# Layer 0's first projections in stages of 128, 128, 256 and three of 512 features; the filter's loads behind a partial sum

## The chip, the cores and the metric

One Trainium2 chip, one core. The time is that of the device from start to end of one execution, in microseconds (us). Before the change it is 1778.45 us, the median of three runs (1774.54 to 1780.24).

## The reference, cut to what matters

A two-layer network over 256 context and 256 latent tokens of width 2048, batch 1, in float32. The part that the change touches is the head of layer 0:

```
mod_l = silu(c) @ ada_w[i] + ada_b[i]            # c: 2048, ada_w[i]: 2048 x 6144
mod_c = silu(c_ctx) @ ada_w[i] + ada_b[i]
sh, sc, gt = split(mod, 3)
h = rmsnorm(x, norm_w[i]) * (1 + sc) + sh        # 512 tokens x 2048 features
p = h @ w_in[i]                                  # 2048 x 6688
...                                              # S5, Hyena, retention and GLA branches of p
x = x + gt * (concat(gated branches) @ w_out[i])
```

The Hyena branch also needs a filter that hangs on no token: a small network of three sine layers over 256 positions, times a last weight (`hy_w4`), times a decay, and its transform. After both layers the latent tokens are normed once more and are the output.

## The kernel before, in words

Tokens lie along the free axis: a feature block of 128 is one tile of 128 partitions x 512 tokens. `h` cannot be formed for a feature before its shift and scale are there, and these need all 2048 rows of two columns of `ada_w`, 16.8 MB a section. So layer 0's first 2048 output columns (the inputs of S5, and queries and keys of GLA and retention: eight *units* of 256 columns) are summed in stages over the input features. `STAGES` holds the stages' bounds, in units of 256 features: two of 256, three of 512. In `layer0_qk` (L1298) stage f first makes its `h` tiles (`make_h`, each in a rounded part `hi` and a rest `lo`), and starts the modulation of the next stage as a background generator (`self.bg`, from `ada_feat` and `ada`). Then each unit loads its weights (`wpart` L966: one DMA of 256 rows x 256 columns into a `raw` buffer, a cast on ScalarE to `whi`, a subtraction on VectorE to `wlo`), does 12 matmuls (3 for each of 2 row blocks and 2 column halves, `proj_part` L990) and takes `steps` steps of the background. Stage 0 copies a unit's two sums out of PSUM to `part[n, j]` (ScalarE), later stages add to them (VectorE).

`ada` (L1071) computes both modulations at once. Its stationary operand `sc` has 32 columns, two of them in use, so each result takes 32 of TensorE's 128 columns, and four results stand side by side in PSUM tile `pa`: two sections by two halves of the block (`w = n // 2`, L1076). A DMA of 256 KB brings `nk` row blocks of one section; matmuls are issued after each load in stage 0 and after every fourth load (`GRP0`) else. Each fp32 matmul shows as two instructions in the trace. When all are in, `ada_cols` (L1101) transposes them to columns and adds the bias.

`hy_kf` (L488) makes the filter. Its seven larger loads (four parts of `w4`, two of `dec`, one `kd`) go through SP's queue; the small network's weights go through POOL's queue, its input `hyz` through ScalarE's (`const2` L166). `between` (L1490) runs it ahead of stage 1's units, and S5's loads, parameters and first generated part (`EG`) ahead of stages 2, 3 and 4.

Buffers: nine `raw` of 256 KB, shared by weights and ada loads; six each of `whi` and `wlo`; three PSUM banks `pj` and two `pB`, which units use in turn. A planner sets the order of instructions on each engine ahead of time from its own modelled timeline: what is written later may be issued earlier, and each engine then keeps that order.

Of the kernel before, what the change touches and what calls it, by code (L numbers as in the profile page):

```python
# [10 lines left out]
F32 = mybir.dt.float32  # L11
# [84 lines left out]

STAGES = (0, 1, 2, 4, 6, 8)
GRP, GRP0 = 4, 4
ENG = {'p': 'pp', 'm': 'pv', 'v': 'vv'}
HOW = 'tvtvtvtv'  # L100
# [5 lines left out]
ELF = 9  # L106
EG = (4, 9)
MARK = lambda label: None
# [8 lines left out]
class Net:  # L117
# [370 lines left out]
    def hy_kf(self, i, kfd):  # L488
# [4 lines left out]
        mark(f'hykf{i}')  # L493
        w4 = [self.t2() for _ in range(2)]
        for o in range(2):
            for d in range(2):
                nc.sync.dma_start(w4[o][d * 64:(d + 1) * 64], I['hy_w4'][i][:, (2 * d + o) * 512:(2 * d + o + 1) * 512])
        dec = [self.t2() for _ in range(2)]
        for jt in range(2):
            nc.sync.dma_start(dec[jt], self.C['hydec'][:, jt])  # L500
        kd = self.t2()
        nc.sync.dma_start(kd, self.C['kdft'].rearrange("p a b c -> p (a b c)"))
# [7 lines left out]
        for o in range(2):  # L510
            mark(f'hykf{i}')
            f = {}
# [21 lines left out]
            for ri in range(2):  # L534
                ps = []
# [429 lines left out]

    def wpart(self, src, r0, c0, w, step=True, keep=False):  # L966

        raw = self.raw()[:, :, :w]
        self.nc.sync.dma_start(raw, src[r0:r0 + 256, c0:c0 + w].rearrange("(k p) c -> p k c", p=128))
        if keep:  # L970
            hi, lo = (self.tp.tile([128, 2, 256], F32R, name="m" + t, tag="m" + t, bufs=NM[t])[:, :, :w] for t in 'AB')
        else:
            hi, lo = self.whl('whi')[:, :, :w], self.whl('wlo')[:, :, :w]
        self.nw += 1
        next(self.extra, None)
        self.split(hi, lo, raw, 'v')
        if step:
            self.due += self.rate
            n = int(self.due)
            self.due -= n  # L980
            self.step(n)
        return hi, lo
# [6 lines left out]

    def proj_part(self, W, kq, c0, ps, t0, first, last, step=True):  # L990

        hi, lo = self.wpart(W, kq * 256, c0, 256, step)
        for j in range(2):
            cs = slice(j * 128, (j + 1) * 128)
            o = ps[j][:, t0:]
            for k in range(2):
                xh, xl = self.hh[kq * 2 + k][:, t0:], self.hl[kq * 2 + k][:, t0:]
                self.mm(o, hi[:, k, cs], xh, start=first and k == 0, stop=False)
                self.mm(o, hi[:, k, cs], xl, start=False, stop=False)
                self.mm(o, lo[:, k, cs], xh, start=False, stop=last and k == 1)  # L1000

# [69 lines left out]
    def ada(self, i, cols, n, group, done):  # L1071
# [3 lines left out]
        nc = self.nc  # L1075
        w = n // 2  # L1076
        p = self.ps.tile([128, 512], F32, name="pa", tag="pa", bufs=1)[:, :w]
        src = self.I['ada_w'][i].rearrange("(p k) c -> p k c", k=KT)
# [4 lines left out]
        for m, (k, s, a) in enumerate(loads):  # L1083
# [3 lines left out]
            for dk in range(nk):  # L1087
                for b in range(0, wl, w):
                    todo.append((2 * s + (a + b) // w, k + dk, x[:, dk, b:b + w]))
            if (m + 1) % group == 0:  # L1090
# [3 lines left out]
            if m < len(loads) - 1:  # L1094
                yield
        r = self.sm.tile([128, 256], F32, name="adr", bufs=1)[:, :w]
        self.cp(r, p)
# [3 lines left out]
    def ada_cols(self, r, adab, k0, m):  # L1101

        n = r.shape[1] // 128
        p = self.ps.tile([128, 512], F32, name="pa", tag="pa", bufs=1)
        for s in range(n):
            self.tr(p[:, s * 128:(s + 1) * 128], r[:, s * 128:(s + 1) * 128])
# [191 lines left out]
    def layer0_qk(self, xT, m, adab, vec, rrow, between):  # L1298
# [4 lines left out]
        bounds = STAGES  # L1303
        stage = lambda f: self.ada_feat(0, bounds[f] * 256, (bounds[f + 1] - bounds[f]) * 256, m, adab, 1 if f == 0 else GRP0) \
            if f < ELF else self.ada_feat_el(0, bounds[f] * 256, m, adab, ELENG0)
# [3 lines left out]
        for f in range(last + 1):  # L1309
            kqs = range(bounds[f], bounds[f + 1])  # L1310
            for k in range(2 * kqs[0], 2 * kqs[-1] + 2):
                self.make_h(k, xT[k], m, vec, rrow)
            steps = 0
            if f < last:
                self.bg = stage(f + 1)
                steps = (bounds[f + 2] - bounds[f + 1]) * 16 // (len(units) * len(kqs)) + 1
            between(f)
            for n, (c0, j0, cb) in enumerate(units):
# [3 lines left out]
                mark(f'qk{f}')  # L1322
                for kq in kqs:
                    self.proj_part(W, kq, c0, ps, 0, kq == kqs[0], kq == kqs[-1], False)
                    self.step(steps)
                for j in range(2):
                    if f == 0:
                        part[n, j] = self.t2()
                        self.cp(part[n, j], ps[j])
                    else:  # L1330
                        self.add(part[n, j], part[n, j], ps[j])
                    if f == last:
                        cb(j0 + j, part[n, j])
# [122 lines left out]
    def run(self, out):  # L1456
# [33 lines left out]
        def between(f):  # L1490
            self.cur = 'A'
            if f == 1:
                for _ in hk:
                    pass
            if f == 2:
                self.s5_loads(0)
            if f == 3:
                Ps[0] = self.s5_params(0)
# [142 lines left out]
```

## Time and profile before

| | us |
|---|---|
| median of three runs | 1778.45 |
| the profiled execution | 1779.05 |
| its span in the profile | 1777.1 |
| TensorE (PE) busy | 1718.0, 97% |
| VectorE (DVE) busy | 1234.1, 69% |
| ScalarE (ACT) busy | 738.7, 42% |

The span runs from the first to the last instruction that the profiler saw; the execution's own time is 1.95 us longer. PE is the matmuls, whose ends are modelled: a busy PE need not be at its peak. SP is the engine that issues most DMAs and does nothing else; a `q` behind an engine's name stands for its sequencer, which waits or issues.

### The profile page before, as it was taken

To read this page: it belongs to the slowest core of one execution; us is meant where nothing else is said; L and a number is where in the kernel's file an instruction comes from. 1 tells how busy PE (TensorE), PEld (TensorE's weight loads), DVE (VectorE), ACT (ScalarE), POOL (GpSimd) and SP (SyncE) were. 2 spreads that over 40 slices of the span, in tenths; PEclk is the share of its full clock that TensorE was granted. 3 is DMA by queue.
4 is the path that set the end of the run, shared out by engine and by line. 5 is a ranking of instruction groups with operands and counts; after the bars stand their busy time and mean duration, and the time that the engine had idled before them with its cause. 6 is when DMAs were issued, how large, how long until landed. Compare 5 with 4: busy or idle time off the path is not lost.

```text
span 1777.1 us, 33615 instructions
## 1 busy us (share of the span) xinstructions
PE 1718.0 (97%) x12496; PEld 1403.8 (79%) x12496; DVE 1234.1 (69%) x2495; ACT 738.7 (42%) x1463; POOL 116.3 (7%) x184
## 2 busy tenths in 40 slices
PE   7999999999999999998999999999999999999997
PEld 4656678878777667875789889777997888899997
DVE  2464875569987695965698436558777788578864
ACT  4432253245345344231242433334355555454554
POOL 4000000000000000000023020000000000000133
PEclk9999999999999999999899999899999999999999
DMA  9776865557556486767785474549654435887963
GB/s 291 255 250 171 255 194 169 173 168 215 158 183 190 149 262 218 214 209 238 269 259 169 141 158 156 171 129 312 189 166 123 116 108 159 256 258 233 329 209 122
DMA packets 327995, 355.18 MB, mean 200 GB/s; under 512 B 62912, under 2 KB 247960, under 8 KB 327832
## 3 DMA queue, kind: packets, MB, share of 16 engines
q1 hardware_dynamic: 320672, 343.91, 63.5%
q10 hardware_dynamic: 5112, 8.79, 1.6%
q8 instruction: 98, 1.61, 0.4%
q0 software_dynamic: 2048, 0.34, 0.1%
q14 instruction: 65, 0.53, 0.1%
HBM read 316.11 MB, written 36.83 MB: 199 GB/s over the span
## 4 chain that ended last, share of the span: by engine, by line
PE 79%; DMA 10%; DVE 5%; ACT 2%; issue 2%; SPq 1%; POOL 0%; ACTq 0%; DVEq 0%
PE pj L199 34%; PE pj L1043 20%; PE pB L199 10%; PE pA L199 7%; PE pa L199 4%; DMA raw<-in_w_in_dram 3%; DMA raw<-in_ada_w_dram 2%; PE pB L203 2%; DVE mA L184 1%; PE pA L886 1%; DMA kd<-mA 1%; PE pB L1043 1%; DVE acc L196 1%; DVE wlo L184 1%; PE pA L203 1%
## 5 line engine op out<-in xcount | busy, mean ns | idle before, releaser
L199 PE MATMUL pj<-hs,whi 128*128 128x512 f32 (+1 forms) x2496 | 665.2, 354 | 3.3 <-ACT whi L957 3.1
L957 ACT CAST whi<-raw 128x512 fp32r<-128x512 f32 (+1 forms) x536 | 331.3, 621 | 677.9 <-DMA raw<-in_w_in_dram 298.5
L184 DVE TENSOR_TENSOR wlo<-raw,whi 128x512 fp32r<-128x512 f32 (+1 forms) x536 | 373.1, 702 | 276.6 <-ACT whi L957 259.6
L199 PEld LDWEIGHTS pj<-hs,whi 128*128 128x128 f32 x2496 | 430.0, 190 | 85.7 <-issue 19.3
L1043 PE MATMUL pj<-whi,hs 128*128 128x256 f32 (+1 forms) x2368 | 453.3, 288 | 0.5 <-ACT tr L1426 0.4
L199 PE MATMUL pj<-hs,wlo 128*128 128x512 f32 (+1 forms) x1248 | 439.8, 355 | 0.9 <-DVE wlo L184 0.9
L1043 PEld LDWEIGHTS pj<-whi,hs 128*128 128x128 f32 x2368 | 370.4, 189 | 22.1 <-issue 19.6
L1043 PE MATMUL pj<-wlo,hs 128*128 128x256 f32 (+1 forms) x1184 | 337.5, 285 | 0.0
L199 PEld LDWEIGHTS pj<-hs,wlo 128*128 128x128 f32 x1248 | 235.3, 189 | 43.1 <-issue 11.3
L1043 PEld LDWEIGHTS pj<-wlo,hs 128*128 128x128 f32 x1184 | 223.3, 189 | 5.0 <-issue 4.7
L184 DVE TENSOR_TENSOR mA<-mA 128x512 f32<-128x512 f32 (+6 forms) x342 | 180.8, 557 | 29.3 <-DMA mA<-rq 10.9
L196 DVE SCALAR_TENSOR_TENSOR acc<-raw,sc,acc 128x512 f32<-128x512 f32 x210 | 155.5, 762 | 8.1 <-DMA raw<-in_ada_w_dram 7.5
L199 PE MATMUL pA<-mA 128*64 128x64 f32 (+4 forms) x892 | 119.3, 298 | 5.5 <-DMA mA<-in_s_glu_w_dram 5.1
L199 PE MATMUL pa<-raw,sc 128*32 128x256 f32 (+1 forms) x1152 | 97.0, 371 | 7.6 <-DMA raw<-in_ada_w_dram 6.6
L199 PE MATMUL pB<-hs,whi 128*128 128x512 f32 x320 | 103.6, 403 | 0.1
L199 PE MATMUL pB<-mB 64*64 64x128 f32 (+4 forms) x896 | 95.3, 297 | 8.1 <-DVE mB L184 6.5
L199 PEld LDWEIGHTS pA<-mA 128*64 128x64 f32 (+2 forms) x892 | 75.1, 159 | 27.7 <-issue 15.5
L177 ACT COPY mA<-pA 128x512 f32<-128x512 f32 (+3 forms) x130 | 52.4, 427 | 85.5 <-PE pA L199 44.2
L199 PEld LDWEIGHTS pB<-mB 64*64 64x64 f32 (+2 forms) x896 | 61.6, 155 | 29.1 <-issue 12.0
L199 PEld LDWEIGHTS pa<-raw,sc 128*32 128x32 f32 x1152 | 37.8, 110 | 53.0 <-issue 27.2
L184 DVE TENSOR_TENSOR mB<-mB 128x512 f32<-128x512 f32 (+2 forms) x140 | 66.2, 511 | 18.4 <-ACT mB L301 12.6
L199 PEld LDWEIGHTS pB<-hs,whi 128*128 128x128 f32 x320 | 59.3, 189 | 19.3 <-issue 5.7
(225 smaller groups left out, 1562.3 us busy)
## 6 DMA issues: line engine op xcount, KB each, us to landing
raw<-in_ada_w_dram SPq DMA_DIRECT2D x384, 256.0 KB, 3.8
raw<-in_w_in_dram SPq DMA_DIRECT2D x384, 256.0 KB, 3.7
raw<-in_w_out_dram SPq DMA_DIRECT2D x128, 256.0 KB, 3.3
raw<-in_w_in_dram SPq DMA_DIRECT2D x32, 272.0 KB, 3.3
mB<-kfd SPq DMA_DIRECT2D x24, 256.0 KB, 5.1
mB<-in_ctx_dram SPq DMA_DIRECT2D x16, 256.0 KB, 5.8
mB<-in_x_dram SPq DMA_DIRECT2D x16, 256.0 KB, 6.2
kfd<-mA SPq DMA_DIRECT2D x16, 256.0 KB, 2.8
```

The costliest lines, as they stand in the source:

```text
L177: self.nc.scalar.copy(out, in_)
L184: (self.nc.vector if eng == 'v' else self.nc.gpsimd).tensor_tensor(out, a, b, op=op)
L196: self.nc.vector.scalar_tensor_tensor(out, in0, scalar, in1, op0=op0, op1=op1)
L199: self.nc.tensor.matmul(out, lhsT, rhs, start=start, stop=stop)
L203: self.nc.tensor.transpose(out, in_, self.K['ident'][:p, :p])
L886: nc.tensor.matmul(o, a_, b_, start=part == 0 and q < per, stop=part == 2, skip_group_check=True)
L957: self.nc.scalar.copy(hi, x)
L1043: mm = lambda a, b, start, stop: self.nc.tensor.matmul(o, a, b, start=start, stop=stop, skip_group_check=per > 1)
```

## The change

`STAGES` is now in units of 128 features: two stages of 128, one of 256, three of 512. A stage of 128 has one row block, so `wpart` and `proj_part` get the number of row blocks `nk` (1 or 2) and the first of them `k0`; a unit of such a stage loads 128 KB and does 6 matmuls. `ada` for 128 features takes `w` = 128 (not 64), one result a section (`np_` = 1), so two results of 64 PSUM rows, and its DMA brings four row blocks of 128 columns. `ada_cols` has a case for 64 rows. `steps`, `between` and `EG` follow the new numbers: the filter is now run ahead of stage 2, S5's three parts ahead of stages 3, 4 and 5, each in front of the same features as before. In `hy_kf` the tiles of the seven loads of layer 0 are first written, one column each, with a copy from `self.first`, which is `part[HOLD, 0]` with `HOLD` = 1, the first sum of unit 1 in stage 0. The loads then follow that copy.

```
-STAGES = (0, 1, 2, 4, 6, 8)
+STAGES = (0, 1, 2, 4, 8, 12, 16)
+HOLD = 1
-EG = (4, 9)
+EG = (5, 9)
...
         w4 = [self.t2() for _ in range(2)]
+        dec = [self.t2() for _ in range(2)]
+        kd = self.t2()
+        if i == 0:
+            for x in w4 + dec + [kd]:
+                self.cp(x[:, :1], self.first[:, :1], 'v')
...
-    def wpart(self, src, r0, c0, w, step=True, keep=False):
-        raw = self.raw()[:, :, :w]
-        self.nc.sync.dma_start(raw, src[r0:r0 + 256, c0:c0 + w].rearrange("(k p) c -> p k c", p=128))
+    def wpart(self, src, r0, c0, w, step=True, keep=False, nk=2):
+        raw = self.raw()[:, :nk, :w]
+        self.nc.sync.dma_start(raw, src[r0:r0 + 128 * nk, c0:c0 + w].rearrange("(k p) c -> p k c", p=128))
...
-    def proj_part(self, W, kq, c0, ps, t0, first, last, step=True):
-        hi, lo = self.wpart(W, kq * 256, c0, 256, step)
+    def proj_part(self, W, kq, c0, ps, t0, first, last, step=True, k0=0, nk=2):
+        hi, lo = self.wpart(W, kq * 256 + k0 * 128, c0, 256, step, nk=nk)
...
-        w = n // 2
-        p = self.ps.tile([128, 512], F32, name="pa", tag="pa", bufs=1)[:, :w]
+        w = max(n // 2, 128)
+        np_ = n // w
+        p = self.ps.tile([128, 512], F32, name="pa", tag="pa", bufs=1)[:64 * np_, :w]
...
-                    todo.append((2 * s + (a + b) // w, k + dk, x[:, dk, b:b + w]))
+                    todo.append((np_ * s + (a + b) // w, k + dk, x[:, dk, b:b + w]))
...
+        if r.shape[0] == 64:
+            self.tr(p[:, :64], r)
+            b = adab[:, k0:k0 + 17:16][:, :, None].to_broadcast([128, 2, 2])
+            self.add(m[:, :, k0], p[:, :64].rearrange("p (j w) -> p j w", w=32)[:, :, 0:2], b)
+            return
...
-            kqs = range(bounds[f], bounds[f + 1])
+            ks = range(bounds[f], bounds[f + 1])
+            nk = min(len(ks), 2)
...
-                steps = (bounds[f + 2] - bounds[f + 1]) * 16 // (len(units) * len(kqs)) + 1
+                steps = (bounds[f + 2] - bounds[f + 1]) * 8 // (len(units) * (len(ks) // nk)) + 1
...
+                        self.first = part[HOLD, 0] if n >= HOLD else None
...
-            if f == 1:
+            if f == 2:
                 for _ in hk:
                     pass
```

## Rows read from the trace of the kernel before

**Rows 1.** Page, part 1: busy us (share of the span) x instructions.
```profile
PE 1718.0 (97%) x12496; PEld 1403.8 (79%) x12496; DVE 1234.1 (69%) x2495; ACT 738.7 (42%) x1463; POOL 116.3 (7%) x184
```
**Rows 2.** Windows: length, busy PE, PEld, DVE, ACT, POOL; clock, DMA share, GB/s.
```profile
20.00:30.00 10.00, 9.70 (x124) 6.73 (x118) 3.13 (x9) 4.36 (x8) 5.70 (x12) 1.00 1.04 317
30.00:40.00 10.00, 8.09 (x73) 4.97 (x75) 4.83 (x14) 3.11 (x7) 0.98 (x2) 1.00 1.01 271
```
**Rows 3.** Timeline of PE: start us, us, line, operation, tiles, shape, count [idle before].
```profile
21.60 0.66 PE L199 MATMUL pa<-raw,sc 128*32 128x128 f32 x16
22.78 0.63 PE L199 MATMUL pa<-raw,sc 128*32 128x128 f32 x8
...
32.44 0.63 PE L199 MATMUL pa<-raw,sc 128*32 128x128 f32 x8 [0.21 <-DMA raw<-in_ada_w_dram]
...
34.34 1.26 PE L199 MATMUL pa<-raw,sc 128*32 128x128 f32 x16 [0.58 <-DVE acol L196]
...
36.54 1.28 PE L199 MATMUL pj<-hs,whi 128*128 128x512 f32 x3
...
53.36 1.10 PE L199 MATMUL pa<-raw,sc 128*32 128x128 f32 x30
...
99.56 1.98 PE L199 MATMUL pA<-mA 128*128 128x512 f32 x4
```
**Rows 4.** Waits of PE, 27 to 120 us: total us, times, longest us.
```profile
PE pj L199 <- ACT whi L957: 2.0, 2, 1.3
PE pa L199 <- DMA raw<-in_ada_w_dram: 1.7, 4, 0.8
```
**Rows 5.** Page, part 3: DMA queue, packets, MB, share of 16 engines.
```profile
q1 hardware_dynamic: 320672, 343.91, 63.5%
...
q0 software_dynamic: 2048, 0.34, 0.1%
```
**Rows 6.** Timeline of DVE, scaling of the first two feature blocks.
```profile
34.81 1.66 DVE L196 SCALAR_TENSOR_TENSOR tr<-hs,acol,mA 128x256 f32<-128x256 f32 x4
```
**Rows 7.** Timeline of ACT, 27 to 45 us.
```profile
27.96 0.59 ACT L177 COPY mA<-pA 128x512 f32<-128x512 f32 x1 [1.37 <-PE pA L199]
...
37.22 0.62 ACT L957 CAST whi<-raw 128x512 fp32r<-128x512 f32 x1 [0.19 <-DMA raw<-in_w_in_dram]
44.06 0.55 ACTq L166 DMA_DIRECT2D mA<-const_hyz_dram  x1
```
**Rows 8.** Timeline of SP's queue, the filter's loads among others.
```profile
28.94 0.56 SPq L497 DMA_DIRECT2D mA<-in_hy_w_dram  x1
...
35.96 0.47 SPq L497 DMA_DIRECT2D mA<-in_hy_w_dram  x1
...
41.75 0.46 SPq L502 DMA_DIRECT2D mA<-const_kdft_dram  x1
43.58 0.37 SPq L969 DMA_DIRECT2D raw<-in_w_in_dram  x1
```
**Rows 9.** Chain of waits that ended last: start us, us, what.
```profile
35.96 8.08 DMA mA<-in_hy_w_dram
...
54.45 2.98 PE pj L199 x12
...
111.68 3.97 DMA raw<-in_ada_w_dram
```
**Rows 10.** Groups by line and shape, 0 to 120 us: busy, mean ns | idle before.
```profile
L184 DVE TENSOR_TENSOR wlo<-raw,whi 128x512 fp32r<-128x512 f32 x21 | 14.5, 690 | 29.7 <-ACT whi L957 29.3 <-PE pa L199 0.3
L957 ACT CAST whi<-raw 128x512 fp32r<-128x512 f32 x21 | 13.0, 619 | 42.3 <-DMA raw<-in_w_in_dram 35.5 <-DMA mA<-in_hy_w_dram 6.8
L196 DVE SCALAR_TENSOR_TENSOR hs<-tr,mod,hs 128x256 fp32r<-128x256 f32 x16 | 6.7, 474 | 0.0
L184 DVE TENSOR_TENSOR mB<-mB,pj 128x512 f32<-128x512 f32 x8 | 5.4, 685 | 2.3 <-PE pj L199 2.3
L196 DVE SCALAR_TENSOR_TENSOR acol<-mod,vec 128x2 f32<-128x2 f32 x8 | 0.8, 156 | 0.1
```

More of the change, by code (lines that the diff above doesn't have):

```diff
@@ L497, in hy_kf @@
                 nc.sync.dma_start(w4[o][d * 64:(d + 1) * 64], I['hy_w4'][i][:, (2 * d + o) * 512:(2 * d + o + 1) * 512])
-        dec = [self.t2() for _ in range(2)]
         for jt in range(2):
             nc.sync.dma_start(dec[jt], self.C['hydec'][:, jt])
-        kd = self.t2()
         nc.sync.dma_start(kd, self.C['kdft'].rearrange("p a b c -> p (a b c)"))
@@ L972, in wpart @@
         else:
-            hi, lo = self.whl('whi')[:, :, :w], self.whl('wlo')[:, :, :w]
+            hi, lo = self.whl('whi')[:, :nk, :w], self.whl('wlo')[:, :nk, :w]
         self.nw += 1
@@ L995, in proj_part @@
             o = ps[j][:, t0:]
-            for k in range(2):
-                xh, xl = self.hh[kq * 2 + k][:, t0:], self.hl[kq * 2 + k][:, t0:]
+            for k in range(nk):
+                xh, xl = self.hh[kq * 2 + k0 + k][:, t0:], self.hl[kq * 2 + k0 + k][:, t0:]
                 self.mm(o, hi[:, k, cs], xh, start=first and k == 0, stop=False)
                 self.mm(o, hi[:, k, cs], xl, start=False, stop=False)
-                self.mm(o, lo[:, k, cs], xh, start=False, stop=last and k == 1)
+                self.mm(o, lo[:, k, cs], xh, start=False, stop=last and k == nk - 1)
     def proj_t(self, W, c0, ncol, t0, cb, step=True):
@@ L1095, in ada @@
                 yield
-        r = self.sm.tile([128, 256], F32, name="adr", bufs=1)[:, :w]
+        r = self.sm.tile([128, 256], F32, name="adr", bufs=1)[:64 * np_, :w]
         self.cp(r, p)
@@ L1303, in layer0_qk @@
         bounds = STAGES
-        stage = lambda f: self.ada_feat(0, bounds[f] * 256, (bounds[f + 1] - bounds[f]) * 256, m, adab, 1 if f == 0 else GRP0) \
+        stage = lambda f: self.ada_feat(0, bounds[f] * 128, (bounds[f + 1] - bounds[f]) * 128, m, adab, 1 if f == 0 else GRP0) \
             if f < ELF else self.ada_feat_el(0, bounds[f] * 256, m, adab, ELENG0)
@@ L1309, in layer0_qk @@
         for f in range(last + 1):
-            kqs = range(bounds[f], bounds[f + 1])
-            for k in range(2 * kqs[0], 2 * kqs[-1] + 2):
+            ks = range(bounds[f], bounds[f + 1])
+            nk = min(len(ks), 2)
+            for k in ks:
                 self.make_h(k, xT[k], m, vec, rrow)
@@ L1322, in layer0_qk @@
                 mark(f'qk{f}')
-                for kq in kqs:
-                    self.proj_part(W, kq, c0, ps, 0, kq == kqs[0], kq == kqs[-1], False)
+                for k in ks[::nk]:
+                    self.proj_part(W, k // 2, c0, ps, 0, k == ks[0], k == ks[-nk], False, k % 2, nk)
                     self.step(steps)
@@ L1491, in between @@
             self.cur = 'A'
-            if f == 1:
+            if f == 2:
                 for _ in hk:
                     pass
-            if f == 2:
+            if f == 3:
                 self.s5_loads(0)
-            if f == 3:
+            if f == 4:
                 Ps[0] = self.s5_params(0)
```

## The prediction

> **What bounds the kernel now.** The page's engine row comes first: TensorE (PE) is busy 97% of the span [rows 1], so the 1777.1 us end later or sooner only with what PE has to do and with where it stands idle. The change touches layer 0's first projections alone, so I then read the start in windows of 10 us: from 20 to 40 us the 16 DMA engines are full (shares 1.04 and 1.01) at 317 and 271 GB/s, and the granted clock is 1.00, the level of 2.4 GHz [rows 2]. PE's timeline shows what this leaves: the last pieces of the first ada block (the modulation of features 0 to 255) go through PE at 32.44 us, the first projection matmul starts at 36.54 [rows 3]. In the waits of PE from 27 to 120 us there is hardly anything else: 2.0 us for casts of weights (the longest 1.3) and 1.7 for ada loads [rows 4]. So before 36.5 us the bound is bytes that must land ahead of the first matmul; behind it, PE's own work. A change here gains what it moves out of the first zone, and pays in full for what it adds to the second.
>
> **The start.** The first block now waits for 8 loads of 256 KB in place of 16, 2.1 MB less. At the 317 GB/s of its stretch that is 6.6 us, so the last pieces would land for a matmul at 25.8 us, not 32.44. Against it: rows of 128 floats make packets of 512 bytes, where now they have 1024. No row isolates that size. From both sides: the main queue's packets take 63.5% of 16 x 1777.1 us over 320672, 56 ns for a mean of 1072 bytes, and the software queue's 0.1% over 2048, some 14 ns for 166 bytes [rows 5]. The straight line between gives 30 ns for 512 bytes, 60 for two of them against 54 for one of 1024: 11% dearer, 0.7 us on these 2.1 MB. The ends are nothing at all, and a packet of 512 priced as one of 1072 bytes, which would eat all 6.6 us. I take 0.7, as both rows lie near that line.
>
> Then the ada matmuls themselves. Each writes 32 of PE's 128 columns, and strips of 32 columns work beside each other: 8 instructions on two strips take 0.63 us, 16 on four strips 0.66, and 30 on four strips (eight after another in each) 1.10 [rows 3]. So a strip takes one more instruction each (1.10 - 0.65) / 4 = 0.11 us, whatever the others do. A block of 256 uses four strips (two sections by two halves), a block of 128 two: `np_` is 1. One new load is 8 instructions in one strip, 4 rounds more than now, 0.44 us behind the last landing. The way from there to the first feature scaling is 34.81 - 32.44 = 2.37 us [rows 3, 6]. New: 25.8 + 0.7 + 0.44 + 2.37 = 29.3. The other input, the row of 1/rms, is copied at 27.96 for 0.59 us [rows 7], ready at 28.6, so it doesn't bind but caps the gain at 6.2. The first projection matmul follows as now, 1.73 us behind: 31.0 for 36.54. **Gain 5.5 us** (0 to 6.2).
>
> **What moves behind the start.** The other half of the first ada block is now stage 1's background, in groups of four loads between projection matmuls. A group is 32 instructions as now, but on two strips: 16 rounds, 1.10 + 8 x 0.11 = 2.0 us. Two groups, **4.0 us added** to PE where it has no idle time [rows 4]. The ends: some of it slips ahead of the first matmul, as 16 instructions of the next block do now at 34.34 [rows 3], 2.0 us; or the strips do not overlap at all (a rival below), 7.7. The 256 block keeps its four strips, and the 512 blocks are unchanged.
>
> **The filter's loads.** Seven loads, 1.3 MB (4.1 us at 317 GB/s), stand now in SP's queue from 28.94 to 42 us among weights and ada loads [rows 8]. The hold puts them behind unit 1's partial sum. They are needed late: the filter's first 512-wide product runs at 99.56 [rows 3], so nothing is late for them. What they cost now is seen in PE's longest wait for a cast, 1.3 us [rows 4]: ACT stood from its cast at 37.22 (0.62 us) to 44.06, when its own load of `hyz` could issue [rows 7]; the chain of waits puts that down to the fourth w4 load, 8.08 us from issue to landing [rows 9], and `hyz` is the eighth load behind it (the SP rows from 35.96 to 43.58 hold the seven between) [rows 8]. With that load out of the full queue I count **1.3 us gained** (0 to 1.3). The added wait: SP's load waits for a DVE copy of one column, that for ACT's copy of part[1, 0]; behind it on SP stand weight and ada loads. They need buffers that PE frees at about that time, and the eight loads that can be under way hold up to 2.1 MB, 6.6 us of DMA; I cost it at nothing, and at up to 4.1 us (the time of its own bytes) if SP gets there early. Five copies of one column cost DVE at most 0.16 us each, by the nearest row, a 128x2 operation [rows 10].
>
> **One stage more.** 16 more adds of partial sums (0.685 us, 11 us of DVE), 16 half pieces for 8 whole ones in cast and subtraction (a 128x256 DVE operation takes 0.474 where the 128x512 takes 0.690: 16 x 0.474 - 8 x 0.690 = 2.1 us) [rows 10], 8 more SP issues of 0.4 us [rows 8]. All beside PE: DVE is busy 4.83 of 10 us in the stretch from 30 to 40 [rows 2]. Per unit PE takes half of 2.98 us plus 0.5 of ada [rows 9], 2.0; its DVE work in the second block is 2 x 0.685 + 0.474 = 1.84, so the cover is thin there. PSUM banks and the chain from ada to the features come once more; a stage change costs PE nothing to 4.0 us (a wait for an ada load at 111.68, in front of the first 512 block) [rows 9]; here the next block is small, so I take **0.7 us**. The loads of `hy`, `s5` and `EG` keep their place by features, so nothing of theirs moves; POOL's queue is not passed.
>
> **Sum.** -5.5 + 4.0 - 1.3 + 0.7 = -2.1 us. The profiled execution took 1779.05 us, 1.95 outside the span, and lies 0.6 above the median of 1778.45: 1776.95 by its own time, 1776.3 as a median.
>
> **Rivals.**
> *The start's gain stays whole* (25%). The row of 1/rms alone binds (6.2), one ada group slips in ahead of the first matmul (2.0 paid, not 4.0), and with loads held less by PE half of the 4.0 us wait at 111.68 goes: -6.2 + 2.0 - 1.3 - 2.0 = -7.5, 1771.0. For it: 16 instructions of the next block's ada run ahead of the first matmul already [rows 3]. Against: PE has few waits left to save.
> *ACT stands in front of the start* (15%, slower). `hyz` is not held, and with the held loads gone from ahead of it, it may issue on ACT while the 1/rms row and the first features still need ACT. It waits for the eighth load ahead; ACT stood 6.2 us (37.84 to 44.06) for that [rows 7]. Placed before 28.6 us this eats the whole start gain: +4.0 + 0.7 = +4.7, 1783.2. It decides as soon as ACT's queue reaches `hyz` before the copy of the 1/rms row. Against: the planner put two casts ahead of it so far.
> *Strips don't overlap* (10%). Eight instructions in a row go to one strip, where now it is four on two strips in turn. Should those of the other strip wait for all eight, a group takes 32 rounds: 1.10 + 24 x 0.11 = 3.7 us, 1.7 more, 3.4 for two: +1.3, 1779.7. For it in the rows: nothing with such runs exists to look at; against: 16 instructions on four strips took as long as 8 on two [rows 3].
> The Trainium skill bears on this one ("TensorE: Matmul & The Clock Gate", Part 3, The mechanism): it says that matmuls keep strict program order in start and end. Read hard, that rule gives this rival's time; the 0.66 us for 16 instructions shows that four strips do run together, while how far one strip may run ahead of another no row settles.
> *Hold and split do nothing* is inside the forecast: DMA as full as now and the same work on PE give 0.
>
> **Chances.** Forecast 50%, its own range 1772 to 1780. About 0.3%, 5.3 us, is what can be told from no change: faster is under 1773.1, slower over 1783.8. Faster: most of the first rival (0.20) and an edge of the forecast (0.10), since the planner orders all later work anew: 0.30. Slower: half of the second rival (0.08), edges of the others (0.08): 0.16. Within: 0.54. The range 1768 to 1784 leaves out the far ends of both.
>
> **What will show it.** First projection matmul near 31 us (28 to 29 speaks for the first rival, 36 for the second); groups of 32 ada instructions in the first stage at 2.0 us (3.7: the third); hy loads on SP behind about 33 us, with no standstill of SP there over 4 us; no wait of PE for a cast over 1 us in 31 to 50; start of the 512 blocks some 2 us ahead of now. I am wrong if PE waits for weights over 4 us in the first two stages, or if a difference arises behind layer 0's projections.

## The result, and the profile after

The changed kernel takes 1801.64 us (median of 4 runs, 1800.47 to 1803.39) where the kernel before takes 1779.35 beside it (4 runs, 1774.54 to 1782.01): ratio 1.0111, 95% interval 1.0087 to 1.0134. It is slower by 1%. 1776.3 was forecast with a range of 1768 to 1784, so the prediction is wrong in sign, and the range does not hold the time.

The profiled execution took 1802.67 us, 23.6 more than that of before. The page's engine rows, against [rows 1] (the span is 23.7 us longer):

```profile
PE 1731.2 (96%) x12497; PEld 1408.8 (78%) x12497; DVE 1248.4 (69%) x2524; ACT 743.3 (41%) x1473; POOL 110.2 (6%) x184
```

PE is busy 13.2 us longer with one instruction more, and the rest of the 23.7, 10.5 us, is idle time of PE. Where it is lost shows best in ACT's casts of the weights, each part of which is cast once in either kernel. At equal amounts cast, the changed kernel is 3.4 us ahead at the end of the first part, 10.2 ahead at 49 us of the old time, 8.0 behind at 62, 5.1 at 101, 0.5 at 172, 18.0 at 212, 23.6 at 258, and mostly 20 to 25 from there to 1640 us. So the loss is made inside layer 0's projections, and most of it in 90 us. The windows of that stretch, after (length, busy PE, PEld, DVE, ACT, POOL; granted clock, DMA share, GB/s):

```profile
180.00:200.00 20.00, 20.00 (x93) 14.05 (x92) 11.16 (x23) 4.43 (x10) 0.00 (x0) 1.00 0.14 43
200.00:220.00 20.00, 15.94 (x78) 8.83 (x77) 6.70 (x27) 1.86 (x3) 0.54 (x1) 0.83 0.95 244
...
240.00:260.00 20.00, 20.00 (x111) 14.55 (x110) 19.88 (x42) 7.35 (x13) 0.00 (x0) 1.00 0.76 234
260.00:280.00 20.00, 16.50 (x87) 12.37 (x86) 14.12 (x33) 8.23 (x19) 0.31 (x3) 0.83 0.27 73
```

The same windows of before:

```profile
180.00:200.00 20.00, 20.00 (x122) 13.50 (x121) 15.08 (x66) 4.04 (x7) 0.00 (x0) 1.00 0.80 254
200.00:220.00 20.00, 20.00 (x108) 12.04 (x108) 18.88 (x63) 4.47 (x9) 0.00 (x0) 1.00 0.85 272
...
240.00:260.00 20.00, 20.00 (x113) 15.96 (x112) 13.30 (x28) 11.21 (x22) 0.33 (x3) 1.00 0.54 143
260.00:280.00 20.00, 20.00 (x88) 16.21 (x87) 10.08 (x15) 9.46 (x16) 0.00 (x0) 1.00 0.67 209
```

Two things stand out after that before does not have. From 180 to 200 us the DMA engines do almost nothing (0.14), and in the next window PE idles 4.1 us and its granted clock is 0.83, which means part of it at the 1.2 GHz level. And from 240 to 260 DVE is busy 19.88 of 20 us, after which PE idles 3.5 us, again at 0.83. SP's timeline after shows the first of the two (start, us, operation, count):

```profile
174.19 8.29 SPq L1091 DMA_DIRECT2D raw<-in_ada_w_dram  x3
193.44 0.33 SPq L547 DMA_DIRECT2D kfd<-mA  x1
194.16 0.33 SPq L548 DMA_DIRECT2D kfd<-mA  x1
...
198.71 2.24 SPq L662 DMA_DIRECT2D mA<-in_s_b_re_dram  x2
201.05 2.42 SPq L547 DMA_DIRECT2D kfd<-mA  x1
...
208.47 1.05 SPq L668 DMA_DIRECT2D mA<-in_s_c_im_dram  x2
209.62 1.40 SPq L1091 DMA_DIRECT2D raw<-in_ada_w_dram  x3
```

SP issues nothing from 182.5 to 193.4, then the filter's stores (`kfd`) and S5's eight loads stand among the weights up to 209.6. In before the last store goes out at 173.4 and S5's first load at 168.0:

```profile
168.03 3.31 SPq L658 DMA_DIRECT2D mA<-in_s_b_re_dram  x2
...
173.45 1.41 SPq L544 DMA_DIRECT2D kfd<-mA  x1
```

So the filter and everything behind it are 30 us late. The reader can follow that back. POOL's first small load of the filter after, and the load that stands nine places ahead of it in POOL's queue:

```profile
28.69 0.52 POOL L256 DMA_DIRECT2D mB<-in_norm_w_dram  x1 [17.09 <-PE pA L200]
...
33.26 1.01 POOL L467 DMA_DIRECT2D mA<-in_hy_b_dram  x2
```

and before:

```profile
11.97 1.02 POOL L466 DMA_DIRECT2D mA<-in_hy_b_dram  x2
```

PE's first product of the filter's small net is at 88.07 after, where it was at 67.9:

```profile
88.07 0.64 PE L200 MATMUL pA<-mA 33*64 33x256 f32 x2
```

The held tiles `w4`, `dec` and `kd` come out of the same turning set of buffers `mA` as the filter's small rows, and are taken ahead of them, so it looks as if their wait for a partial sum held up the rest. The traces speak against that. DVE's first copy into a held tile after, and all five of e2, which has the same hold on the old stages, with POOL's first small load there:

```profile
56.14 0.15 DVE L180 COPY mA<-mB 128x1 f32<-128x1 f32 x1
```

```profile
44.41 0.40 DVE L179 COPY mA<-mB 128x1 f32<-128x1 f32 x5 [0.77 <-ACT mB L177]
```

```profile
12.18 1.02 POOL L466 DMA_DIRECT2D mA<-in_hy_b_dram  x2
```

POOL's small loads after are all issued by 42.4 us, before the first held tile is written, and in e2 they stand where they stood in before. What puts them late after is their place in POOL's queue, behind nine loads of `mB` of which the first waits 17.1 us for PE. The net's other input, `hyz`, is issued at 62.93 (44.06 in before [rows 7]), later by about as much as the net, which follows 25 us behind it. For `hyz`, which comes 5 us after the last copy, the traces do not tell whether the hold kept it back. The hold does move the net: without it, in e1 below, the net is at 67.6. But it did so by the order that the planner made with it, not by keeping POOL's loads waiting; why that order came out so is not shown.

The copies also show that the hold lies one stage later than the description of the change has it. The filter is written behind stage 1's units, which add to the partial sums in place, so the copy from `part[1, 0]` follows the second stage's sum (56.14). In e2, and in e9, where the filter stands one stage earlier, it follows the first (44.41 and 39.53).

The second thing, on DVE after, from 251 to 269 us: S5's products (`cbr`, `cbi`, `mA`) stand among the weights' lower halves (`wlo`), the partial sums (`mB`) and the feature scaling of the last block (`tr`, `hs`):

```profile
251.48 1.89 DVE L185 TENSOR_TENSOR wlo<-raw,whi 128x512 fp32r<-128x512 f32 x3
253.28 0.68 DVE L185 TENSOR_TENSOR mA<-mA 128x512 f32<-128x512 f32 x1
...
254.04 0.68 DVE L185 TENSOR_TENSOR mA<-cbi,mA 128x512 f32<-128x512 f32 x1
...
255.24 1.28 DVE L185 TENSOR_TENSOR mB<-mB,pB 128x512 f32<-128x512 f32 x2
...
261.53 2.45 DVE L197 SCALAR_TENSOR_TENSOR tr<-hs,acol,mA 128x256 f32<-128x256 f32 x6
...
268.57 2.46 DVE L197 SCALAR_TENSOR_TENSOR hs<-tr,mod,hs 128x256 fp32r<-128x256 f32 x6
```

In before the last product that is written to `cbi` starts at 217.5, 17 us ahead of that block's first scaling column (`acol`, 234.6); after, at 249.1 against 258.2.

**An account for PE.** At the moment at which ACT casts the last part of these projections PE has done the same instructions in every kernel (1541 or 1542 records; 1501 in e17, where some of S5's products come later). So the time of that cast can be split into idle time and work. Before, all instructions:

```profile
0.00:275.10 275.10, 260.01 (x1541) 172.49 (x1542) 158.41 (x394) 104.61 (x208) 22.15 (x49) 1.00 0.77 235
```

and those on tile `pa`, the conditioning, alone:

```profile
0.00:275.10 275.10, 51.98 (x648) 23.20 (x648) 1.24 (x10) 1.67 (x5) 1.00 0.77 235
```

After, all:

```profile
0.00:298.50 298.50, 276.27 (x1542) 178.94 (x1543) 170.80 (x423) 106.55 (x217) 22.10 (x49) 0.98 0.70 216
```

and on `pa` alone:

```profile
0.00:298.50 298.50, 64.24 (x649) 28.69 (x649) 1.34 (x10) 1.88 (x6) 0.98 0.70 216
```

23.4 us more: 7.1 idle (22.2 against 15.1), 12.3 conditioning, 4.0 the rest. The groups by shape up to that moment say which conditioning. After:

```profile
L200 PE MATMUL pj<-hs,whi 128*128 128x512 f32 x240 | 83.4, 424 | 2.1 <-ACT hs L1258 1.3 <-DVE hs L197 0.8
L200 PE MATMUL pa<-raw,sc 128*32 128x256 f32 x384 | 41.0, 397 | 5.4 <-DMA raw<-in_ada_w_dram 2.6 <-DVE mod L185 1.5 <-issue 1.1
L200 PE MATMUL pa<-raw,sc 128*32 128x128 f32 x256 | 21.2, 278 | 0.3 <-DVE mod L185 0.3
```

Before: 80.0, 34.2 and 15.9 us for the same counts. The 128-wide ones cost 5.3 more, the 256-wide ones 6.8, and the `whi` matmuls on `pj` 3.4, while the `wlo` ones on `pj` cost 1.7 less (47.2 against 48.9). Some of this is the lower clock: from 213 to 219.5 us, at a granted clock of 0.50, 8 and twice 4 of the 256-wide instructions took 1.79, 1.07 and 0.98 us, and a `whi` matmul on `pj` 665 ns, against 407 from 222 to 232.

### The profile page after: what moved, and what is told of

It reads as the page before. It is cut to its first block, busy times and chain, and to the rows that moved or that the text cites. A ratio compares the mean times of both kernels' runs of the same rounds, so it can differ in the third digit from the quotient of the medians.

```text
span 1800.8 us, 33678 instructions
## 1 busy us (share of the span) xinstructions
PE 1731.2 (96%) x12497; PEld 1408.8 (78%) x12497; DVE 1248.4 (69%) x2524; ACT 743.3 (41%) x1473; POOL 110.2 (6%) x184
## 4 chain that ended last, share of the span: by engine, by line
PE 78%; DMA 9%; DVE 6%; ACT 3%; issue 2%; SPq 1%; ACTq 0%; DVEq 0%
PE pj L200 31%; PE pj L1047 21%; PE pB L200 9%; PE pA L200 7%; PE pa L200 5%; DMA raw<-in_w_in_dram 2%; DVE mA L185 2%; PE pA L890 1%; DVE wlo L185 1%; PE pB L1047 1%; PE pB L204 1%; DMA raw<-in_ada_w_dram 1%; DMA raw<-in_w_out_dram 1%; PE pA L204 1%; DVE mB L185 1%
## 5 line engine op out<-in xcount | busy, mean ns | idle before, releaser
L961 ACT CAST whi<-raw 128x512 fp32r<-128x512 f32 (+2 forms) x544 | 333.6, 615 | 706.4 <-DMA raw<-in_w_in_dram 333.8
L185 DVE TENSOR_TENSOR wlo<-raw,whi 128x512 fp32r<-128x512 f32 (+2 forms) x544 | 375.9, 697 | 269.2 <-ACT whi L961 247.3
L200 PE MATMUL pa<-raw,sc 128*32 128x256 f32 (+1 forms) x1152 | 107.6, 370 | 9.9 <-DMA raw<-in_ada_w_dram 6.8
L200 PEld LDWEIGHTS pa<-raw,sc 128*32 128x32 f32 x1152 | 42.8, 110 | 60.3 <-issue 36.1
L185 DVE TENSOR_TENSOR mB<-mB 128x512 f32<-128x512 f32 (+2 forms) x140 | 64.8, 503 | 17.1 <-ACT mB L302 12.2
```

The lines of the kernel that those rows point to most:

```text
L185: (self.nc.vector if eng == 'v' else self.nc.gpsimd).tensor_tensor(out, a, b, op=op)
L200: self.nc.tensor.matmul(out, lhsT, rhs, start=start, stop=stop)
L961: self.nc.scalar.copy(hi, x)
```

## The experiments

**Theory D** (the one I came to; its first part is called A below): the hold pushes the filter back, S5's loads take the filter's tiles and come 30 us late, stop the weights, and S5's DVE work meets the last block. Its first part falls with e1 and e2. **Rivals**: B, the split costs by itself; C, the filter's stores on SP are the price. All numbers at a glance; last cast, idle and conditioning as in the account above (for every kernel the same two window rows), last store and first S5 load from SP's or POOL's timeline:

| kernel | last filter store | S5's first load | last cast | PE idle | on `pa` | ratio (95%) |
|---|---|---|---|---|---|---|
| before | 173.4 | 168.0 | 275.1 | 15.1 | 52.0 | 1 |
| after | 203.6 | 198.7 | 298.5 | 22.2 | 64.2 | 1.0111 (1.0087-1.0134) |
| e1 split, no hold | 192.2 | 188.7 | 287.3 | 17.5 | 58.3 | 1.0120 (1.0091-1.0148) |
| e2 hold only | 184.1 | 179.9 | 279.6 | 19.3 | 51.1 | 1.0030 (1.0009-1.0050) |
| e3 stores on POOL | 202.0 | 199.6 | 296.8 | 22.2 | 63.8 | 1.0141 (1.0115-1.0166) |
| e4 net first | 178.1 | 172.7 | 279.2 | 12.7 | 58.0 | 1.0028 (1.0008-1.0047) |
| e7 old blocks, filter late | 190.2 | 183.3 | 284.9 | 23.2 | 53.1 | 1.0072 (1.0031-1.0113) |
| e9 filter a block earlier | 168.0 | 163.4 | 281.1 | 15.1 | 56.8 | 1.0042 (1.0008-1.0076) |
| e11 e9, net first | 163.9 | 158.9 | 287.4 | 16.6 | 62.1 | 1.0072 (1.0041-1.0102) |
| e12 e11, no hold | 155.3 | 151.3 | 278.3 | 14.3 | 57.9 | 1.0030 (0.9998-1.0063) |
| e10 net first, no hold | 177.1 | 171.7 | 277.9 | 13.5 | 59.9 | 1.0002 (0.9984-1.0019) |
| e13 before, net first | 170.9 | 165.1 | 271.7 | 12.0 | 53.7 | 0.9986 (0.9967-1.0005) |
| e14 after, S5 first | 197.7 | 28.2 | 286.7 | 17.7 | 60.4 | 1.0050 (1.0031-1.0070) |
| e17 stores, S5 on POOL | 207.4 | 194.8 | 285.6 | 16.6 | 61.9 | 1.0056 (1.0036-1.0077) |
| e16 e4, S5 first | 177.6 | 29.0 | 280.9 | 13.5 | 60.5 | 1.0045 (1.0028-1.0063) |
| e15 before, S5 first | 176.6 | 28.4 | 286.9 | 21.4 | 56.5 | 1.0062 (1.0041-1.0083) |
| e24 e13, S5 first | 173.6 | 29.0 | 284.1 | 17.7 | 56.9 | 1.0039 (1.0023-1.0056) |
| e23 groups of two | 205.3 | 201.1 | 298.7 | 24.2 | 63.1 | 1.0138 (1.0108-1.0168) |

The delay of the last cast agrees with the ratio to about 4 us (1779 x (ratio - 1)), but for e1, where the ratio stands for 21 us and the cast is 12 late; its profiled execution ended 17 us behind that of before. So most of the difference is made up to the last cast, but single executions move behind it: that of e10 won back 6 us there and that of e12 lost 8, so differences of a few us between rows say nothing.

### The two halves alone

e1: the change without the copies that hold the tiles.

```diff
-        if i == 0:
-            for x in w4 + dec + [kd]:
-                self.cp(x[:, :1], self.first[:, :1], 'v')
```

> The new stages without the hold (the filter's seven loads follow no partial sum). The changed kernel loses its time late: level with before until 171 us, 18.4 us behind at 231, 23.4 at 278. Theory A, the hold pushes the whole filter back and that collides later: without it 1775 to 1780, the filter's first matmul near 68 us. Theory B, the split alone puts the filter late in the plan (in SP's planned order the last filter stores still stand behind 105 ada loads, 97 before): 1790 to 1803, with SP standing in front of a filter store near 180 to 200 us.

e2: the kernel before with the hold alone (tiles taken early, the five copies, `self.first = part[1, 0]`), on the old blocks.

> The hold alone, on the old stages of 256, 256 and three of 512. Theory A (the hold is the cause): 1793 to 1803, POOL's small filter loads from 12 us to behind 45, the filter's first matmul from 67.9 to 85 or later, SP standing over 8 us at a filter store. Theory B (the split is the cause): 1776 to 1783.

e1 came to 1796.97 us, e2 to 1782.85. Neither half alone is the change, and theory A falls: without the hold the loss stays, though POOL's loads are back at 12.0 us and the net at 67.6, and with the hold alone most of it is gone. Both times lie where theory B had put them: the split alone brings about the whole loss, and it does so with a late filter (last store at 192.2). The stop of SP that B expected with it is not there: in e1 SP's longest wait at a store from 160 to 205 us is 2.6 us. What the slow kernels share is a late filter, not a held one.

### The stores

```diff
-                nc.sync.dma_start(kfd[o, 0, ri], y)
+                (nc.gpsimd if i == 0 else nc.sync).dma_start(kfd[o, 0, ri], y)
```

(the second store likewise)

> The changed kernel with layer 0's eight stores of the filter's transform issued by POOL and not by SP; nothing else. Theory C, the price is SP standing 10.9 us in front of a store whose data are not ready, with weight and ada loads behind it: the DMA share from 180 to 200 us rises from 0.14 to over 0.6 and the time falls to 1780 to 1790. Rival: the price is the pile of VectorE's work at 252 to 268 us (S5's parameters together with the last block), which stays as it is: 1795 to 1803.

1801.61 us, no better than the change: rival C falls. SP stands as long (15.6 us), now at a weight load that waits for a conditioning group on PE.

### The filter's order

e4: the changed kernel, with the small net written ahead of the held tiles.

```diff
+        h = self.hy_filters(i) if i == 0 else None
         w4 = [self.t2() for _ in range(2)]
...
-        h = self.hy_filters(i)
+        if i:
+            h = self.hy_filters(i)
```

> The changed kernel, with the filter's small net (its POOL loads, hyz, its matmuls) written ahead of the held tiles, so that the hold can reach the seven large loads alone. If the hold does harm by taking the small net along (it is allocated behind the held tiles): POOL's small loads are back near 12 us and the time is 1774 to 1782. If the late place of the seven loads or the split itself is the cause: 1793 to 1803.

e7: the kernel before, with the filter started at the third block (512 features) and not the second (256): no split, no hold.

```diff
-            if f == 1:
+            if f == 2:
                 for _ in hk:
                     pass
-            if f == 2:
                 self.s5_loads(0)
```

> The kernel before, with the filter run ahead of stage 2 and not stage 1; stages and loads as they were, no hold. Theory D: S5's loads get their tiles only where the filter's last ones come free, S5's parameters follow some 30 us behind those loads, and if that work of VectorE reaches the last block's scaling, PE waits. In five runs so far the first S5 load was issued 3.5 to 5.4 us ahead of the filter's last store and the first parameter 29 to 31 us behind that load. D expects: filter's last store behind 185 us, S5's first load some 4 us ahead of it, its first parameter 30 us later, and 1783 to 1800 us. Rival, the narrow stages themselves cost the time: 1775 to 1780.

e4 takes 1781.40 us: three quarters of the loss (1.0028 against 1.0111) come back with split and hold in place, by the order in which the filter's tiles are taken. The edit also moves the seven held loads, from 56.3 to 99.2 us; in e10, without the hold, they go out at 97.1, so there the hold changes little. e7 takes 1791.53: a late filter costs 13 us on the old blocks, with nothing else of the change. Together these put the loss on the filter's place.

e9, e11 and e12 look whether earlier still is better: the changed kernel with the filter at 128 features (`f == 1` for `f == 2`), then with the net first as well, then without the hold.

> The changed kernel, hold and all, with the filter run ahead of stage 1 (features 128 to 255) and not stage 2. D expects the filter's last store before 182 us, S5's first load before 178, and 1774 to 1783 us. Rival, the narrow stages or the hold cost the time whatever the filter does: 1793 to 1803.

> As the run before (filter ahead of stage 1), and its small net ahead of the held tiles. D expects the filter's last store earlier still, before 172 us, and 1771 to 1779: the stages' own balance (first projection matmul 2.5 to 3 us earlier) is then all that is left. Rival, the narrow stages cost PE more at their two boundaries than the start gives: 1780 to 1786, as in the fourth run.

> As the run before, without the hold. If the hold does anything of its own once the filter's place is right: 2 us or more apart from that run, slower, since the seven loads then stand among the first weights. By D: within 3 us of it.

1787.91, 1792.40 and 1784.34 us. Earlier still was not better: e11 is dearer than e4 (1.0072 against 1.0028, the intervals just overlap), and its first block of 512 starts 9 us later than in after (122.6 for 113.2). That the filter's products meet the small blocks there is my reading; no run isolates it.

### What a late filter costs through S5

e14: the changed kernel, held and late as it is, but S5's loads issued ahead of the filter.

```diff
             if f == 2:
+                self.s5_loads(0)
+                for _ in self.extra:
+                    pass
                 for _ in hk:
                     pass
-            if f == 3:
-                self.s5_loads(0)
```

> The changed kernel with its split, its held tiles and its late filter (last filter store planned where it was, near 203 us), but with S5's eight parameter loads taken ahead of the filter: they are issued between 20 and 60 us, on tiles of their own turn, and no longer stand behind the filter's last tiles. Theory D (the late filter costs time because S5's loads take its tiles, so that S5's parameters fall 30 us later onto the last block): S5's loads come in before 70 us, its parameter work on VectorE no longer stands in 240 to 260 us, and most of the 22 us is gone: 1780 to 1788. Rival E (the late filter costs by itself, by its two stores and its products beside the second last block): 1797 to 1803, as the changed kernel. Rival F (only the pile on VectorE at 250 us goes, the standstill of SP's queue at 182 to 198 us stays, since the kernel that issued the stores elsewhere still had it): 1793 to 1797.

e17: the changed kernel with stores and S5's loads on POOL's queue (`self.nc.gpsimd` for `self.nc.sync` in `s5_loads` and in the stores, layer 0 only).

> The changed kernel, with the filter's eight stores and S5's eight loads issued on POOL's queue in place of SP's. SP carries only the weights, so no store or S5 load can stand ahead of a weight load; the filter and S5's parameters are as late as in the changed kernel. If what costs is the order of SP's queue (18 of the 23 us), the weights go on between 200 and 210 us and the time is 1783 to 1788. If the nine weight buffers that the conditioning groups hold are what stops the stream, the stop stays from 182 to 198 us and the time is 1795 to 1803. By theory D in its full form S5's late parameters still meet the last block, so at least 5 us over the kernel before remain in either case.

1789.43 and 1792.54 us: each takes back about half. e14's last store is still at 197.70:

```profile
197.70 0.32 SPq L548 DMA_DIRECT2D kfd<-mA  x1
```

and its windows have no idle PE between 180 and 240 us:

```profile
180.00:200.00 20.00, 20.00 (x95) 14.80 (x97) 14.25 (x37) 5.04 (x12) 0.54 (x1) 1.00 0.31 108
200.00:220.00 20.00, 20.00 (x130) 12.88 (x119) 12.06 (x60) 3.21 (x6) 0.00 (x0) 1.00 0.79 249
220.00:240.00 20.00, 20.00 (x120) 12.30 (x118) 18.71 (x62) 7.23 (x14) 0.00 (x0) 1.00 0.78 246
240.00:260.00 20.00, 17.24 (x101) 12.57 (x101) 20.00 (x43) 8.53 (x19) 0.00 (x0) 1.00 0.55 165
```

So S5's place behind the filter is worth about half of the loss, not most of it, as theory D had it; DVE is still full at 250 us. What is left in e14 beside e10 is 4 us of idle PE and a slower rest. In e17 SP stops just as long with nothing but weights in its queue, and its longest wait from 172 to 200 us names the reason:

```profile
SPq L973 <- PE pa L200: 15.6, 1, 15.6
```

A weight load waits for a buffer that conditioning loads hold until their group runs on PE, in the changed kernel at 197.61. With stores and S5's loads out of its queue the weights go on, S5's work moves behind the last block (its first `s5prm` at 242.2, where DVE is 19 of 20 us busy up to 280), and half of the price is left.

e23: the changed kernel with groups of two loads.

```diff
-GRP, GRP0 = 4, 4
+GRP, GRP0 = 4, 2
```

> The changed kernel with layer 0's conditioning products issued after every second load in place of every fourth, so that a waiting group holds two of the nine weight buffers and not four. If the held buffers are what stops the stream at 182 to 198 us, that stop shrinks to below 8 us and the time falls to 1785 to 1795. If the order of SP's queue and the late filter behind it decide, the stop stays and the time is 1799 to 1806. Smaller groups also make more short pieces on TensorE: up to 5 us more for the conditioning products in either case.

1802.63 us: the stop stays, 11.2 us on the same wait. It is not the size of the groups that holds the buffers; why the planner put that group at 197 us is open.

### What the split is worth in the right order

e10: e4 without the held copies. e13: the kernel before with the net first, the edit of e4 on the old blocks.

> The changed kernel without the held tiles, and with the filter's small net ahead of its large loads (as e4_net_first, which with the held tiles came to 1781.4). This has the split alone, with the filter's tiles in the order in which they are needed. If the held tiles cost nothing where the net is not behind them: 1780 to 1784, level with e4_net_first within 0.2%. If the early loads of 1.7 MB still get in the way of the first partial sum, as the hold supposes: 1784 to 1790. If the hold itself cost time: 1774 to 1779.

> The kernel before with one change: the filter's small net (its loads on POOL's queue and three small products) is written ahead of its large tiles. Old blocks, no held tiles. If the net's place is worth nothing by itself, 1777 to 1781, and the split's own cost is what e10_split_net_no_hold showed, about nothing. If the net's place gains, 1768 to 1774, and the split costs that much, hidden in e10. If it costs (filter loads issued only at 97 us as in e10): 1783 to 1788, and the split gains.

1781.74 us against 1780.7 for e10, 1774.58 against 1778.96 for e13. e10 shows no difference from before, and its PE never idles from 180 to 280 us:

```profile
180.00:200.00 20.00, 20.00 (x111) 14.15 (x110) 15.55 (x59) 4.25 (x9) 0.00 (x0) 1.00 0.79 224
200.00:220.00 20.00, 20.00 (x121) 11.49 (x119) 18.75 (x74) 6.03 (x11) 0.00 (x0) 1.00 0.87 282
...
260.00:280.00 20.00, 20.00 (x88) 16.19 (x87) 10.60 (x16) 11.09 (x18) 0.00 (x0) 1.00 0.70 213
```

Its conditioning groups up to the last cast (277.9 us):

```profile
L200 PE MATMUL pa<-raw,sc 128*32 128x256 f32 x384 | 36.7, 386 | 3.1 <-DMA raw<-in_ada_w_dram 1.9 <-PE pB L200 0.7 <-PE pA L200 0.5
L200 PE MATMUL pa<-raw,sc 128*32 128x128 f32 x256 | 21.2, 278 | 0.6 <-DMA raw<-in_ada_w_dram 0.3 <-DVE mod L185 0.3
```

So of the 12.3 us on `pa`, the 128-wide blocks' 5.3 belong to the split in any order, and of the 6.8 on 256-wide ones 2.5. e10 pays that with less idle time (13.5) and a shorter rest, and ends 2.8 us behind at the last cast. The hold in the right order (e4 against e10) is 0.26% dearer and the split (e10 against e13) 0.16%; the intervals overlap or touch, so neither is told from nothing. e13 is the fastest kernel seen, but its interval holds 1: no version is shown to beat the kernel before.

### S5's loads early in a good order

> The changed kernel with its split and its held tiles, the filter's small net ahead of them, and S5's eight loads ahead of the filter. Theory D: the last delays behind the filter are gone, so what is left is the split by itself: 1777 to 1782, level with the kernel before or up to 0.2% from it. Rival G (the four tiles that S5's loads hold from 20 us on are missing to the filter, which then ends later): 1784 to 1790. If the split is worth its 2.9 us at the start: 1774 to 1777.

> The kernel before with one change: S5's eight parameter loads are issued ahead of the filter's loads (planned after the third weight load) in place of behind the filter's last tiles. If bringing S5's loads early gives time only where they were late: 1777 to 1782. If 1 MB of loads ahead of the first weights costs, as e16_net_s5_first against e4_net_first (+7 us) suggests: 1783 to 1790. If the kernel before already suffers from S5's late loads: 1768 to 1774.

> The kernel before with both orders: S5's loads first, then the filter's net, then the filter's large tiles. It is run to see whether the old blocks leave anything to gain from the order of these loads. If the effects add, it is the sum of e13_before_net and e15_before_s5_first; if early loads cost: 1783 to 1790; if there is a gain: under 1774.

1789.01, 1790.29 and 1786.59 us. What helps the late filter costs elsewhere: 0.62% on the kernel before. e15's windows show where: eight more loads stand among the first weights.

```profile
20.00:40.00 20.00, 17.09 (x179) 11.23 (x180) 7.53 (x22) 6.92 (x13) 6.66 (x13) 0.91 1.04 261
40.00:60.00 20.00, 12.64 (x89) 8.64 (x89) 1.39 (x2) 4.15 (x8) 0.00 (x0) 0.82 1.03 253
```

PE idles 7.4 us of 40 to 60, with the DMA engines full, 5.9 of it for casts of weights, and the window's granted clock is 0.82. So bytes ahead of the first projections can cost, as the hold supposed; but for the filter's own loads in that place no run shows a cost (holding them alone, in e2, gained nothing).

## Why the prediction was wrong, point by point

**The step that failed** is a sentence without a number: "The loads of `hy`, `s5` and `EG` keep their place by features, so nothing of theirs moves; POOL's queue is not passed." With it goes "They are needed late ... so nothing is late for them", the hold costed at nothing. Both looked at where the calls stand in the loop over features and at the first 512-wide product (99.56). Neither asked where the planner would set the filter's steps once the blocks had changed. POOL's loads moved from 11.97 to 33.26, the net by 20 us, the last store and S5's loads by 30. By e4 against after, the written order of the filter's tiles is worth 0.8% (1.0028 against 1.0111), three quarters of the loss. That a late filter is enough was shown (e7), and that half goes by way of S5's loads (e14, e17). The split alone is enough to make it late (e1: nothing held, net at 67.6, last store at 192.2, ratio 1.0120), the hold alone does little (e2: 184.1, 1.0030). Why the planner sets the filter later with the narrow stages is open; it is not forced by them, as e10 differs from e1 only in the written order and has its last store at 177.1 and 1.0002.

**The start, 5.5 us.** It came to 2.9. PE's timeline after, against [rows 3]:

```profile
28.39 1.53 PE L200 MATMUL pa<-raw,sc 128*32 128x128 f32 x16
...
30.79 2.93 PE L200 MATMUL pa<-raw,sc 128*32 128x128 f32 x40 [0.26 <-DVE mod L185]
33.65 0.73 PE L200 MATMUL pj<-hs,whi 128*128 128x512 f32 x2
35.01 1.06 PE L200 MATMUL pa<-raw,sc 128*32 128x128 f32 x8
...
38.52 1.53 PE L200 MATMUL pa<-raw,sc 128*32 128x128 f32 x16
```

The last pieces end at 29.92, where the prediction's own figures give 27.6 (25.8 + 0.7 + 0.63 + 0.44). They were two loads' worth in one go, and the landing was later than counted: from 20 to 30 us the full engines (share 1.04) moved 269 GB/s against 317 [rows 2], so a byte was 18% dearer, where 11% had been counted for packets half as long; other loads stand in both windows too. Then 40 instructions of the next block stand in front of the first projection for 2.93 us; its input was ready at 32.73, so that took another 0.9.

**Strips, +4.0 us.** The second block's 64 instructions took 2.93 + 1.06 + 1.53 = 5.5 us, and over all 128-wide ones the price is 5.3. The term was sized about a quarter too low. The third rival (no overlap) wanted 1.98 for 16 instructions (0.66 + 12 x 0.11), full overlap 1.10; 1.53 is 12 rounds, half way. (For no overlap at all the prediction has 7.7 us for two groups; its own 1.10 + 24 x 0.11, twice, is 7.5.) The Trainium skill ("TensorE: Matmul & The Clock Gate", Part 3, The mechanism) says that matmuls start and end in program order. The trace speaks against the hard reading that the prediction gave it, by which no strip runs ahead and 16 instructions take the 1.98: 1.53 leaves room for a strip to begin its eight some four rounds before the other has done its own. The order of ends it can't test, since the profile models them.

**The filter's loads, -1.3 us.** The wait went, but not by the hold, so this was luck: in PE's waits from 27 to 120 us there is none left for a cast of weights, against 2.0 us [rows 4], and there is none in e1 either, where the seven loads are not held and go out from 29.0 to 44.8. In e2, the hold on the old stages, 0.7 us of it is left.

**One stage more, +0.7 us.** Mis-sized: at the change from 128 to 256 features PE idles 1.46 us for `mod` and 0.25 for `hs`, 1.7 in all. The upper end of 4.0 us, which the first rival uses too, was misread: the 3.97 us at 111.68 [rows 9] are a DMA in the chain of waits, and all that PE waited for ada loads from 27 to 120 us is 1.7, at most 0.8 at a time [rows 4].

**"512 blocks are unchanged".** The 256-wide instructions cost 2.5 us more in the best order and 6.8 as built. PE works at them in more and shorter pieces (counted in the records up to 300 us: 42 and 47 uninterrupted runs, where before has 38), and one short piece costs as much as a longer one (below). Part of the 6.8 is the lower clock, as above.

**The sum behind the filter.** With these sizes (-2.9, +5.3, -1.3, +1.7, +2.5) the split would be +5.3 at the last cast, against -2.1; e10 shows +2.8 and no difference in the end. So without the failed step the class "within 0.3%" would have held for the split (e10, 1.0002), and just about for split and hold together (e4, 1.0028, its interval reaching to 1.0047); a gain of 2.1 us no kernel with the split shows. At 172 us the changed kernel looks level in weights cast, but from 60 us on PE had worked 17.4 us on `pA`, the filter's products, against 26.0: a debt of 8.6 us that a count of weights alone hides.

**The rivals.** None was the cause. The second had the right kind of thought, a load set free to take another place, but looked at `hyz` in front of the start, where it did no harm; it went 18.9 us later instead (62.93 for 44.06), as the whole net did. "I am wrong if a difference arises behind layer 0's projections" did not come true: it arose inside them.

## What to carry to other kernels

Where a planner sets the order, a change can move a chain of work that it does not touch: look up in the new order where that chain's steps stand before you cost it at nothing. The place of a side chain among the main work can be worth more than the change at hand, here 1%; look at when its last step ends, not at when its first large one starts. When a step is late, compare its time with that of the wait that you blame: here the late loads ran 23 us before the held tiles were written. To compare two traces in a stretch where one engine is full, take the moment at which that engine has done the same instructions in both, and split the time into idle and work.

## What the runs showed of the hardware

Column strips of PE overlap, but by the times here one strip runs only about four instructions ahead of another (16 on two strips in runs of eight: 1.53 us; 40: 2.93, where 0.65 and 20 rounds of 0.11 would give 2.85). That is an estimate from the lengths of these groups.

A piece of conditioning on four strips costs in steps. Timeline of PE after, 256-wide instructions:

```profile
197.61 0.63 PE L200 MATMUL pa<-raw,sc 128*32 128x256 f32 x6
199.23 1.05 PE L200 MATMUL pa<-raw,sc 128*32 128x256 f32 x10
203.19 1.48 PE L200 MATMUL pa<-raw,sc 128*32 128x256 f32 x18
207.59 0.62 PE L200 MATMUL pa<-raw,sc 128*32 128x256 f32 x2
```

Two instructions cost as much as six, so cutting the work into smaller pieces between other matmuls is not free.

Where PE stood idle for 3.5 to 7.4 of 20 us (200 to 220 and 260 to 280 us after, 40 to 60 in e15) the granted clock of the window was 0.82 or 0.83. Closer by: from 206 to 213 us after, PE was busy 3.0 of 7 us at a clock of 0.99, and from 213 to 219.5 it was busy 6.4 of 6.5 us at 0.50, the level of 1.2 GHz. So idle time was paid a second time, in slower matmuls (665 ns for 407, above). The amount of idle time alone does not tell when: 2.8 us in e14's window from 240 to 260 went with 1.00, 2.9 in e15's from 20 to 40 with 0.91.
